# Log gates of a gated linear attention kept as one fp32 array, with fp32 running sums and decay weights built from total minus sum

## The chip, the cores and the metric

The kernel runs on one core of one Trainium2 chip. The metric is the device time of one execution in microseconds, as the median of several runs. The engines are TensorE (PE in the rows; PEld is its weight load), VectorE (DVE), ScalarE (ACT), GpSimd (POOL) and SyncE (SP, which here only issues transfers).

## The reference, cut to what matters

One layer of a backbone over 512 latent tokens, width 1024, with 256 context tokens in front. Of the layer, this case touches the gated linear attention (GLA) branch: 4 heads, key width 128, value width 256, run over the tokens forwards and backwards. For each direction there is a log gate per token and key channel, and the state is decayed by it:

```python
def log_gate(lr, up, bias):
    pre = (lr @ up + bias).astype(jnp.float32)
    return heads(jax.nn.log_sigmoid(pre) / GLA_TAU, GLA_DK)
...
b = jnp.cumsum(gi, axis=1)
b_last = b[:, -1]
...
S_new = jnp.exp(b_last)[..., None] * S + jnp.einsum(
    'bshk,bshv->bhkv', ki * jnp.exp(b_last[:, None] - b), vi)
```

The context tokens give only a start state for each direction, with the same weighting of the keys: `k * exp(b[:, -1:] - b)`. The other branch (a state-space scan, SSD), the merge, the output projection and a SwiGLU block follow, and are not changed.

## The kernel before, in words

Tokens stand in six tiles of 128: four of the latent stream, two of the context. Every large product of the layer is done as three products in fp32r (a matmul format of reduced precision): each weight block is loaded in fp32 (`raw_...`, three buffers in rotation, issued on SP's queue), split into a high part by ACT (`whi_...`, line 188) and a remainder by DVE or POOL (`wlo_...`, line 189), and multiplied as high times high, high times low and low times high. `some_ada` slips a modulation block between them: it is loaded through the same three buffers and summed by POOL (lines 341 to 345).

The order of instructions on each engine is laid down when the program is built: a planner simulates the engines and places each instruction by when it expects it to be ready. Instructions issued through `Early` (the matmuls and transposes of the chains) or under `high_priority` go ahead of others. On the chip, each engine then runs its list in that order and waits where an input is late.

**The gates** (lines 466 to 480). For 2 directions times 6 token tiles, PE forms `pre` in [token, channel]; ACT does three passes over 128x512 (absolute value, exponential, logarithm), and DVE one (line 474), which leaves the log gate `ge`. Then DVE rounds it to fp32r (`gh`, line 477) and forms the remainder (`gl`, line 478), and both go by SP's queue to a DRAM array `gdr`. Around these lines in time stand the value and gate projections of head 0 (`r_v`, `r_r`) on PE, the time steps of the SSD branch (`dtT`, `dt_...`, `cum`, `suf`, `cumT`, lines 488 to 567), which run as a chain through PE, DVE and ACT, and the query and key projections of head 1 (`l_q`, `l_k`).

**The chain of a GLA head** (`gla_chain`, once for each of 4 heads). For each direction, POOL's queue loads the head's columns of `gh` and `gl` (`g`, line 592). With 0/1 triangle matrices (`mkr`) PE forms three things, each as a pair of products with the high and the low part: the running sums in [channel, token] for the four latent tiles (`gc`, line 598), the suffix sums in [token, channel] for three latent tiles (`kx`) and for two context tiles (`ky`). ACT exponentiates the suffix sums (lines 613, 614) and DVE multiplies them with `kt`, the keys in [token, channel] (lines 615, 616), which gives the weighted keys `kd`. `kt` was made in `gla_proj_qk` by six transposes of the keys `kT` (line 441) and two copies (line 442). Then the states `S` are formed from `kd` and the values, the within-tile attention in seven levels (`eq`, `ek`, `lv`, `att`), and at the end the outputs `o`, which need `S` and `att`.

PE works on the projections of head h+1 while the chain of head h runs. Results of the chain pass through four PSUM banks in rotation (`sm_bank`); `g` and `kd` of one direction take turns in two buffers (tags `cva`, `cvt`).

Of the kernel before, what the change touches and what calls it, by code (L numbers as in the profile page):

```python
# [24 lines left out]
DK = 128  # L25
# [4 lines left out]
TAU = 16.0  # L30
# [13 lines left out]
M_ID, M_LE, M_GE, M_GT, M_LT, M_ONE = range(6)  # L44
# [85 lines left out]
def hybrid_layer_kernel(ctx: ExitStack, tc: tile.TileContext, x, xc, wts, vec, rows, up, msk, lvl, out):  # L130
    nc = tc.nc
# [8 lines left out]
    sml = ctx.enter_context(tc.tile_pool(name="sml", bufs=2))  # L140
    ps = ctx.enter_context(tc.tile_pool(name="ps", bufs=4, space=PSUM))
    dr = ctx.enter_context(tc.tile_pool(name="dr", bufs=1, space=DRAM))
# [4 lines left out]
    def sm_bank(name):  # L147
        return ps.tile([P, 512], F32, tag="sm", name=name)
# [4 lines left out]
    mkr = cst.tile([P, 5, P], F32R, name="mkr")  # L153
# [6 lines left out]
    ident = idt[:, :]  # L160
# [64 lines left out]
    with tc.tile_pool(name="st", bufs=1) as st:  # L225
# [77 lines left out]
        for i in range(6):  # L303
# [5 lines left out]
            for half in range(2):  # L309
                pt = sm_bank(f"xT_{i}_{half}")  # L310
                for k in range(4):
                    kk = half * 4 + k
# [7 lines left out]
    pj = mix.enter_context(tc.tile_pool(name="pj", bufs=2))  # L320
    ch = mix.enter_context(tc.tile_pool(name="ch", bufs=1))
# [105 lines left out]
    def gla_proj_qk(h):  # L427
        lat, _ = proj_cols(("q", h), False)
        qT = pj.tile([P, SEQ], F32, tag="p3", name=f"qT_{h}")
        nc.scalar.activation(qT, lat, AF.Copy, scale=float(DK) ** -0.5)  # L430
        big = pj.tile([P, 3072], F32, tag="x12", name=f"kv_{h}")
        vt = big[:, 0:1536].rearrange("p (i c) -> p i c", c=DV)
        kt = big[:, 1536:2304].rearrange("p (i c) -> p i c", c=DK)
        kT = big[:, 2304:3072]
        lat, cx = proj_cols(("k", h), True)
        nc.scalar.activation(kT[:, 0:SEQ], lat, AF.Copy)
        nc.vector.tensor_copy(kT[:, SEQ:NT], cx[:, 0:CTX])
        for b, i0, n in ((0, 0, 4), (1, 4, 2)):
            pt = sm_bank(f"kt_{h}_{b}")
            for i in range(n):  # L440
                nc.tensor.transpose(pt[:, i * P:(i + 1) * P], kT[:, (i0 + i) * P:(i0 + i + 1) * P], ident)
            nc.scalar.activation(kt[:, i0:i0 + n, :], pt[:, 0:n * P].rearrange("p (i c) -> p i c", c=DK), AF.Copy)
        return qT, vt, kt, kT

    def gla_proj_vr(h, qT, vt, kt, kT):
        banks = proj_rows(lambda kh: ("v", h, kh), 6)
        for b in range(3):
            nc.scalar.activation(vt[:, 2 * b:2 * b + 2, :], banks[b].rearrange("p (i c) -> p i c", c=DV), AF.Copy)
        banks = proj_rows(lambda kh: ("r", h, kh), 4)
        rw = pj.tile([P, 4, DV], F32, tag="p4", name=f"rw_{h}")  # L450
        for b in range(2):
            rv = rw[:, 2 * b:2 * b + 2, :]
            pv = banks[b].rearrange("p (i c) -> p i c", c=DV)
            with tc.issue_after(ln_end.ins) if h == 0 else nullcontext():
                nc.scalar.activation(rv, pv, AF.Tanh, scale=0.5)
            nc.vector.scalar_tensor_tensor(rv, rv, 1.0, pv, ALU.add, ALU.mult)
            nc.gpsimd.tensor_tensor(rv, rv, gnh.unsqueeze(1).to_broadcast([P, 2, DV]), ALU.mult)
        return qT, vt, kt, kT, rw

    def gla_proj(h):  # L460
        return gla_proj_vr(h, *gla_proj_qk(h))


    gdr = dr.tile([P, 2, 2, 6, 512], F32, name="gdr")

    for d in range(2):
        for i in range(6):
            pt = sm_bank(f"pre_{d}_{i}")
            nc.tensor.matmul(pt, MS[d][:, i * P:(i + 1) * P], U[:, d, :], start=True, stop=True)
            e = ch.tile([P, 512], F32, tag="s2", name=f"ge_{d}_{i}", bufs=7)  # L470
            nc.scalar.activation(e, pt, AF.Abs)
            nc.scalar.activation(e, e, AF.Exp, scale=-1.0)
            nc.scalar.activation(e, e, AF.Ln, bias=1.0)
            nc.vector.scalar_tensor_tensor(e, pt, 0.0, e, ALU.min, ALU.subtract)
            gh = ch.tile([P, 512], F32R, tag="z", name=f"gh_{d}_{i}", bufs=4)
            gl = ch.tile([P, 512], F32R, tag="E4", name=f"gl_{d}_{i}", bufs=4)
            nc.vector.tensor_copy(gh, e)
            nc.vector.tensor_tensor(gl, e, gh.bitcast(F32), ALU.subtract)
            nc.sync.dma_start(gdr[:, d, 0, i, :], gh.bitcast(F32))
            nc.sync.dma_start(gdr[:, d, 1, i, :], gl.bitcast(F32))  # L480


    dsh = [P, 6, 64]
# [1 line left out]
    for b, i0, n in ((0, 0, 4), (1, 4, 2)):  # L485
        pt = sm_bank(f"dtT_{b}")
# [9 lines left out]
    e = dt_tile("dt_e")  # L496
# [63 lines left out]
    for d in range(2):  # L560
        pt = sm_bank(f"cumT_{d}")
# [17 lines left out]

    early = Early()  # L580

    def gla_chain(h, qT, vt, kt, kT, rw, oH, oL):
        def s2(name, shape=(P, SEQ)):
            return ch.tile(list(shape), F32, tag="s2", name=f"{name}_{h}", bufs=7)

        cm, kd = [], []
        for d, mc, ms, n0, far, near in ((0, M_LE, M_GT, 0, 4, 5), (1, M_GE, M_LT, 1, 5, 4)):
            tag = ("cva", "cvt")[d]
            gp = []
            for p_ in range(2):  # L590
                gd = pj.tile([P, 6, DK], F32R, tag=tag, name=f"g_{h}_{d}_{p_}")
                nc.gpsimd.dma_start(gd, gdr[:, d, p_, :, h * DK:(h + 1) * DK])
                gp.append(gd)

            pt = sm_bank(f"gc_{h}_{d}")
            for n in range(NCH):
                for p_ in range(2):
                    early.matmul(pt[:, n * P:(n + 1) * P], gp[p_][:, n, :], mkr[:, mc - 1, :], start=(p_ == 0), stop=(p_ == 1))
            c_ = s2(f"gcum{d}")
            nc.scalar.activation(c_, pt, AF.Copy, scale=1.0 / TAU)  # L600
            cm.append(c_)

            px = sm_bank(f"kx_{h}_{d}")
            for p_ in range(2):
                early.matmul(px[:, 0:384], mkr[:, ms - 1, :], gp[p_][:, n0:n0 + 3, :], start=(p_ == 0), stop=(p_ == 1))
            py = sm_bank(f"ky_{h}_{d}")
            o0 = (far - 4) * P
            for p_ in range(2):
                early.matmul(py[:, 0:256], mkr[:, ms - 1, :], gp[p_][:, 4:6, :], start=(p_ == 0), stop=False)
            for p_ in range(2):  # L610
                early.matmul(py[:, o0:o0 + P], mkr[:, M_ONE - 1, :], gp[p_][:, near, :], start=False, stop=(p_ == 1))
            kk = pj.tile([P, 5, DK], F32, tag=tag, name=f"kd_{h}_{d}")
            nc.scalar.activation(kk[:, 0:3, :], px[:, 0:384].rearrange("p (i c) -> p i c", c=DK), AF.Exp, scale=1.0 / TAU)
            nc.scalar.activation(kk[:, 3:5, :], py[:, 0:256].rearrange("p (i c) -> p i c", c=DK), AF.Exp, scale=1.0 / TAU)
            nc.vector.tensor_tensor(kk[:, 0:3, :], kk[:, 0:3, :], kt[:, n0:n0 + 3, :], ALU.mult)
            nc.vector.tensor_tensor(kk[:, 3:5, :], kk[:, 3:5, :], kt[:, 4:6, :], ALU.mult)
            kd.append(kk)

        qd = []
# [595 lines left out]
```

## Time and profile before

| what | value |
|---|---|
| median of 3 runs | 1433.0 us (1431.25 to 1437.1) |
| the profiled execution | 1428.55 us |
| its span, first to last instruction | 1426.7 us |
| mean granted TensorE clock | 0.986 of full speed |
| PE busy | 1349.4 us, 95% of the span |
| DVE / ACT / POOL busy | 881.1 / 496.7 / 476.1 us |
| DMA | 175.49 MB, mean 123 GB/s |

All rows are of the profiled execution, in microseconds from the start of its span. Busy times of PE overlap, since matmuls are pipelined: what one costs is read from the distance between starts, or from the chain of waits, and not from its duration.

### The profile page before, as it was taken

To read this page: it belongs to the slowest core of one execution; us is meant where nothing else is said; L and a number is where in the kernel's file an instruction comes from. 1 tells how busy PE (TensorE), PEld (TensorE's weight loads), DVE (VectorE), ACT (ScalarE), POOL (GpSimd) and SP (SyncE) were. 2 spreads that over 40 slices of the span, in tenths; PEclk is the share of its full clock that TensorE was granted. 3 is DMA by queue.
4 is the path that set the end of the run, shared out by engine and by line. 5 is a ranking of instruction groups with operands and counts; after the bars stand their busy time and mean duration, and the time that the engine had idled before them with its cause. 6 is when DMAs were issued, how large, how long until landed. Compare 5 with 4: busy or idle time off the path is not lost.

```text
span 1426.7 us, 19130 instructions
## 1 busy us (share of the span) xinstructions
PE 1349.4 (95%) x7462; PEld 1146.0 (80%) x7462; DVE 881.1 (62%) x1317; ACT 496.7 (35%) x825; POOL 476.1 (33%) x341
## 2 busy tenths in 40 slices
PE   5888999999998999998999989999889999999997
PEld 3687999889888778876887787778678888888886
DVE  4599757583595588558857975767683343433235
ACT  6464343433434132532332342332333323232222
POOL 1346555245423533343353324114641122100001
PEclk9998999999999999999999999999999999999999
DMA  9375433423422423323322333457423343333331
GB/s 370 123 259 151 128 102 111 126 93 126 122 75 67 141 98 101 97 73 90 104 82 89 96 97 101 158 184 267 135 87 109 113 122 115 120 116 93 100 106 72
DMA packets 71386, 175.49 MB, mean 123 GB/s; under 512 B 6384, under 2 KB 22912, under 8 KB 71168
## 3 DMA queue, kind: packets, MB, share of 16 engines
q1 hardware_dynamic: 57056, 161.11, 34.6%
q0 software_dynamic: 13952, 12.79, 3.8%
q8 instruction: 59, 0.97, 0.3%
q10 hardware_dynamic: 288, 0.36, 0.1%
q14 instruction: 31, 0.25, 0.1%
HBM read 159.37 MB, written 14.87 MB: 122 GB/s over the span
## 4 chain that ended last, share of the span: by engine, by line
PE 66%; DVE 16%; DMA 9%; issue 5%; ACT 2%; POOL 1%; SPq 0%; POOLq 0%; DVEq 0%; ACTq 0%
DMA E<-cdr 6%; PE up L1069 3%; PE gate L1068 3%; PE gate L1069 3%; PE up L1068 3%; PE gate L1067 3%; PE up L1067 3%; DVE E L830 3%; PE db L204 3%; PE db L206 3%; PE db L205 3%; PE lv L577 2%; PE pb_pb L716 2%; PE pb_pb L715 2%; PE pb_pb L717 2%
## 5 line engine op out<-in xcount | busy, mean ns | idle before, releaser
L341 POOL TENSOR_TENSOR raw_ada<-raw_ada,cs 128x1024 f32<-128x1024 f32 x32 | 69.7, 2180 | 265.3 <-DMA raw_ada<-in_wts_dram 230.4
L830 DVE TENSOR_TENSOR E<-E,ebias 128x512 f32<-128x512 f32 x64 | 68.8, 1077 | 51.0 <-DMA E<-cdr 50.8
L343 POOL TENSOR_TENSOR raw_ada<-raw_ada 128x512 f32<-128x512 f32 x64 | 80.0, 1250 | 3.7
L386 PE MATMUL r_z<-whi_z,hH 128*128 128x256 f32 x256 | 74.6, 291 | 5.8 <-DVE z L781 3.0
L388 PE MATMUL r_z<-whi_z,hL 128*128 128x256 f32 x256 | 73.4, 287 | 0.0
L387 PE MATMUL r_z<-wlo_z,hH 128*128 128x256 f32 x256 | 73.0, 285 | 0.0
L1067 PE MATMUL gate<-h2H,whi_gate 128*128 128x512 f32 (+1 forms) x192 | 72.2, 376 | 0.0
L1068 PE MATMUL gate<-h2L,whi_gate 128*128 128x512 f32 (+1 forms) x192 | 72.1, 376 | 0.0
L1069 PE MATMUL gate<-h2H,wlo_gate 128*128 128x512 f32 (+1 forms) x192 | 71.9, 374 | 0.0
L189 POOL TENSOR_TENSOR wlo_xs<-raw_xs,whi_xs 128x1024 fp32r<-128x1024 f32 x16 | 40.6, 2536 | 75.3 <-ACT whi_xs L188 75.3
L1069 PE MATMUL up<-h2H,wlo_up 128*128 128x512 f32 x160 | 63.0, 394 | 0.0
L1068 PE MATMUL up<-h2L,whi_up 128*128 128x512 f32 x160 | 62.4, 390 | 0.0
L1067 PE MATMUL up<-h2H,whi_up 128*128 128x512 f32 x160 | 62.3, 389 | 0.0
L189 DVE TENSOR_TENSOR wlo_down<-raw_down,whi_down 128x1024 fp32r<-128x1024 f32 x18 | 22.1, 1225 | 62.4 <-ACT whi_down L188 62.3
L189 DVE TENSOR_TENSOR wlo_gate<-raw_gate,whi_gate 128x1024 fp32r<-128x1024 f32 x20 | 31.7, 1584 | 45.6 <-ACT whi_gate L188 45.6
L170 POOL TENSOR_TENSOR rr_f<-rv_f,negh 128x1 f32<-128x1 f32 x4 | 2.6, 662 | 168.5 <-DVE rv_f L168 168.5
L386 PE MATMUL r_v<-whi_v,hH 128*128 128x256 f32 x192 | 56.4, 294 | 0.0
L189 POOL TENSOR_TENSOR wlo_z<-raw_z,whi_z 128x1024 fp32r<-128x1024 f32 x16 | 39.6, 2475 | 49.2 <-ACT whi_z L188 36.6
L387 PE MATMUL r_v<-wlo_v,hH 128*128 128x256 f32 x192 | 55.5, 289 | 0.0
L715 PE MATMUL pb_pb<-yT,whi_pb 128*128 128x512 f32 x128 | 55.3, 434 | 0.0
L388 PE MATMUL r_v<-whi_v,hL 128*128 128x256 f32 x192 | 55.3, 288 | 0.0
L205 PE MATMUL db<-wlo_down,fH 128*128 128x512 f32 x142 | 55.3, 389 | 0.0
(479 smaller groups left out, 4446.7 us busy)
## 6 DMA issues: line engine op xcount, KB each, us to landing
raw_ada<-in_wts_dram SPq DMA_DIRECT2D x32, 512.0 KB, 4.0
E<-cdr SPq DMA_DIRECT2D x64, 256.0 KB, 3.5
raw_gate<-in_wts_dram SPq DMA_DIRECT2D x22, 512.0 KB, 3.7
raw_up<-in_wts_dram SPq DMA_DIRECT2D x22, 512.0 KB, 3.5
raw_down<-in_wts_dram SPq DMA_DIRECT2D x22, 512.0 KB, 3.5
aw<-in_wts_dram SPq DMA_DIRECT2D x8, 1024.0 KB, 15.5
raw_xs<-in_wts_dram SPq DMA_DIRECT2D x16, 512.0 KB, 3.5
raw_z<-in_wts_dram SPq DMA_DIRECT2D x16, 512.0 KB, 3.6
```

The lines of the kernel that those rows point to most:

```text
L189: (nc.gpsimd if split_pool[0] else nc.vector).tensor_tensor(lo, raw, hi.bitcast(F32), ALU.subtract)
L205: nc.tensor.matmul(out_, aH, bL, start=False, stop=False)
L341: nc.gpsimd.tensor_tensor(raw, raw, cs[:, :, 0:1].to_broadcast([P, KD, P]), ALU.mult)
L343: nc.gpsimd.tensor_tensor(raw[:, 0:n, :], raw[:, 0:n, :], raw[:, n:2 * n, :], ALU.add)
L386: nc.tensor.matmul(o, hH[:, kk, tk], hi[:, k, :], start=st, stop=False, skip_group_check=True)
L387: nc.tensor.matmul(o, hH[:, kk, tk], lo[:, k, :], start=False, stop=False, skip_group_check=True)
L388: nc.tensor.matmul(o, hL[:, kk, tk], hi[:, k, :], start=False, stop=sp, skip_group_check=True)
L715: nc.tensor.matmul(pt, hi[:, k, cl], aH[:, k, :], start=(k == 0), stop=False)
L830: nc.vector.tensor_tensor(ed, ed, ebias[:, d, n, hh].unsqueeze(2).to_broadcast([P, EH, P]), ALU.add)
L1067: nc.tensor.matmul(pts[kj][:, tk], hi[:, k, :], h2H[:, k, tk], start=(k == 0), stop=False)
L1068: nc.tensor.matmul(pts[kj][:, tk], hi[:, k, :], h2L[:, k, tk], start=False, stop=False)
L1069: nc.tensor.matmul(pts[kj][:, tk], lo[:, k, :], h2H[:, k, tk], start=False, stop=(k == KD - 1))
```

## The change

`gh` and `gl` and their 24 transfers are dropped: `ge` itself is written to `gdr`, which is half as large. Each direction of a head loads one tile `gd` in place of two. The running sums are formed by one fp32 product in place of two fp32r products, for the four latent tiles (`gc`) and now for the two context tiles too (`gx`), all in [channel, token]. The suffix sums `kx` and `ky` are dropped. The weights are exp(total - sum), with the total as a per-channel bias of the exponential, so the five tiles take one exponential each; for the context, two small DVE operations (`tx`) make the bias. The weights are multiplied with `kT` in [channel, token], the five products are transposed on PE (`pk`), and copied by ACT into `kd`. The transposes and copies that made `kt` are dropped.

```diff
-        kt = big[:, 1536:2304].rearrange("p (i c) -> p i c", c=DK)
...
-        for b, i0, n in ((0, 0, 4), (1, 4, 2)):
-            pt = sm_bank(f"kt_{h}_{b}")
-            for i in range(n):
-                nc.tensor.transpose(pt[:, i * P:(i + 1) * P], kT[:, (i0 + i) * P:(i0 + i + 1) * P], ident)
-            nc.scalar.activation(kt[:, i0:i0 + n, :], pt[:, 0:n * P].rearrange("p (i c) -> p i c", c=DK), AF.Copy)
...
-    gdr = dr.tile([P, 2, 2, 6, 512], F32, name="gdr")
+    gdr = dr.tile([P, 2, 6, 512], F32, name="gdr")
...
-            gh = ch.tile([P, 512], F32R, tag="z", name=f"gh_{d}_{i}", bufs=4)
-            gl = ch.tile([P, 512], F32R, tag="E4", name=f"gl_{d}_{i}", bufs=4)
-            nc.vector.tensor_copy(gh, e)
-            nc.vector.tensor_tensor(gl, e, gh.bitcast(F32), ALU.subtract)
-            nc.sync.dma_start(gdr[:, d, 0, i, :], gh.bitcast(F32))
-            nc.sync.dma_start(gdr[:, d, 1, i, :], gl.bitcast(F32))
+            nc.sync.dma_start(gdr[:, d, i, :], e)
...
-            gp = []
-            for p_ in range(2):
-                gd = pj.tile([P, 6, DK], F32R, tag=tag, name=f"g_{h}_{d}_{p_}")
-                nc.gpsimd.dma_start(gd, gdr[:, d, p_, :, h * DK:(h + 1) * DK])
-                gp.append(gd)
-
+            gd = pj.tile([P, 6, DK], F32, tag=tag, name=f"g_{h}_{d}")
+            nc.gpsimd.dma_start(gd, gdr[:, d, :, h * DK:(h + 1) * DK])
+
+            mask = mkr[:, mc - 1, :].bitcast(F32)
+            px = sm_bank(f"gx_{h}_{d}")
+            for n in range(2):
+                early.matmul(px[:, n * P:(n + 1) * P], gd[:, 4 + n, :], mask, start=True, stop=True)
             pt = sm_bank(f"gc_{h}_{d}")
             for n in range(NCH):
-                for p_ in range(2):
-                    early.matmul(pt[:, n * P:(n + 1) * P], gp[p_][:, n, :], mkr[:, mc - 1, :], start=(p_ == 0), stop=(p_ == 1))
+                early.matmul(pt[:, n * P:(n + 1) * P], gd[:, n, :], mask, start=True, stop=True)
...
-            px = sm_bank(f"kx_{h}_{d}")
-            for p_ in range(2):
-                early.matmul(px[:, 0:384], mkr[:, ms - 1, :], gp[p_][:, n0:n0 + 3, :], start=(p_ == 0), stop=(p_ == 1))
-            py = sm_bank(f"ky_{h}_{d}")
-            o0 = (far - 4) * P
-            for p_ in range(2):
-                early.matmul(py[:, 0:256], mkr[:, ms - 1, :], gp[p_][:, 4:6, :], start=(p_ == 0), stop=False)
-            for p_ in range(2):
-                early.matmul(py[:, o0:o0 + P], mkr[:, M_ONE - 1, :], gp[p_][:, near, :], start=False, stop=(p_ == 1))
+
+            col = P - 1 if d == 0 else 0
+            tx = sml.tile([P, 2], F32, tag="gtx", name=f"gtx_{h}_{d}")
+            at = lambda i: px[:, (i - 4) * P + col:(i - 4) * P + col + 1]
+            nc.vector.tensor_scalar(tx[:, 0:1], at(near), 1.0 / TAU, None, ALU.mult)
+            nc.vector.scalar_tensor_tensor(tx[:, 1:2], at(far), 1.0 / TAU, tx[:, 0:1], ALU.mult, ALU.add)
+            ek = pj.tile([P, 5, P], F32, tag=tag, name=f"kw_{h}_{d}")
+            for i, bias in ((near, tx[:, 0:1]), (far, tx[:, 1:2])):
+                nc.scalar.activation(ek[:, i - 1, :], px[:, (i - 4) * P:(i - 3) * P], AF.Exp, bias=bias, scale=-1.0 / TAU)
+            for i in range(3):
+                t0 = (n0 + i) * P
+                nc.scalar.activation(ek[:, i, :], c_[:, t0:t0 + P], AF.Exp, bias=c_[:, t0 + col:t0 + col + 1], scale=-1.0)
             kk = pj.tile([P, 5, DK], F32, tag=tag, name=f"kd_{h}_{d}")
-            nc.scalar.activation(kk[:, 0:3, :], px[:, 0:384].rearrange("p (i c) -> p i c", c=DK), AF.Exp, scale=1.0 / TAU)
-            nc.scalar.activation(kk[:, 3:5, :], py[:, 0:256].rearrange("p (i c) -> p i c", c=DK), AF.Exp, scale=1.0 / TAU)
-            nc.vector.tensor_tensor(kk[:, 0:3, :], kk[:, 0:3, :], kt[:, n0:n0 + 3, :], ALU.mult)
-            nc.vector.tensor_tensor(kk[:, 3:5, :], kk[:, 3:5, :], kt[:, 4:6, :], ALU.mult)
+            for i, n, t0 in ((3, 2, SEQ), (0, 3, n0 * P)):
+                ev = ek[:, i:i + n, :]
+                nc.vector.tensor_tensor(ev, ev, kT[:, t0:t0 + n * P].rearrange("p (i t) -> p i t", t=P), ALU.mult)
+                pk = sm_bank(f"kd_{h}_{d}_{i}")
+                for j in range(n):
+                    early.transpose(pk[:, j * P:(j + 1) * P], ek[:, i + j, :], ident)
+                nc.scalar.activation(kk[:, i:i + n, :], pk[:, 0:n * P].rearrange("p (i c) -> p i c", c=DK), AF.Copy)
             kd.append(kk)
```

## Rows read from the trace of the kernel before

**Rows 1.** The page's busy times: busy us, share, instructions.

```profile
PE 1349.4 (95%) x7462; PEld 1146.0 (80%) x7462; DVE 881.1 (62%) x1317; ACT 496.7 (35%) x825; POOL 476.1 (33%) x341
```

**Rows 2.** Stretches: busy us of PE, PEld, DVE, ACT, POOL; then granted clock, DMA share.

```profile
74.80:92.60 17.80, 17.77 (x141) 17.20 (x139) 17.73 (x24) 14.62 (x28) 9.46 (x8) 1.00 0.81 285
92.60:109.20 16.60, 10.34 (x83) 9.63 (x81) 16.50 (x23) 4.20 (x8) 8.88 (x10) 0.95 0.97 276
109.20:125.00 15.80, 13.78 (x59) 11.83 (x60) 14.16 (x23) 7.99 (x14) 8.84 (x8) 0.73 0.66 193
125.00:430.00 305.00, 301.04 (x1976) 275.98 (x1974) 205.97 (x357) 115.32 (x210) 141.18 (x103) 1.00 0.38 110
```

**Rows 3.** Waits of PE, 55 to 125: total us, times, longest.

```profile
PE l_q L366 <- DVE wlo_q L189: 3.3, 1, 3.3
PE dtT L488 <- DVE ge L474: 2.7, 1, 2.7
PE kt L441 <- DVE cumT L564: 2.0, 1, 2.0
```

**Rows 4.** DVE groups, 74.5 to 109: count, busy us, mean ns, idle before.

```profile
L478 DVE TENSOR_TENSOR gl<-ge,gh 128x512 fp32r<-128x512 f32 x12 | 15.8, 1328 | 0.1
L477 DVE CAST gh<-ge 128x512 fp32r<-128x512 f32 x12 | 8.5, 713 | 0.1
```

**Rows 5.** Timeline of ACT and DVE, 88 to 109: start, us, operation.

```profile
88.66 0.62 ACT L473 ACTIVATE ge<-ge 128x512 f32<-128x512 f32 x1
...
93.11 1.16 ACT L473 ACTIVATE ge<-ge 128x512 f32<-128x512 f32 x2
...
95.80 1.22 DVE L189 TENSOR_TENSOR wlo_r<-raw_r,whi_r 128x1024 fp32r<-128x1024 f32 x1
...
103.06 0.53 ACT L497 ACTIVATE dt_e<-dt_v 128x384 f32<-128x384 f32 x1 [8.79 <-DVE dt_v L489]
...
107.94 1.22 DVE L189 TENSOR_TENSOR wlo_q<-raw_q,whi_q 128x1024 fp32r<-128x1024 f32 x1
```

**Rows 6.** Chain of waits, 109 to 131: start, us on the chain.

```profile
110.01 0.43 PE l_q L361
...
115.01 0.24 PE l_q L362
...
120.98 1.05 PE kt L441 x4
...
128.55 0.23 PE ky L577 x2
...
129.58 0.62 PE gc L577 x6
130.20 0.28 PE l_k L366
```

**Rows 7.** Timeline of PE: eight records of four fp32 products.

```profile
163.41 1.06 PE L577 MATMUL lv<-eq,ek 128*128 128x128 f32 x8
164.23 0.37 PE L388 MATMUL r_v<-whi_v,hL 128*128 128x256 f32 x1
```

**Rows 8.** ACT groups by form: copies of 128x128, biased passes of 128x256.

```profile
L838 ACT ACTIVATE cbs<-cb 128x128 f32<-128x128 f32 x16 | 4.3, 271 | 13.6 <-PE cb L577 13.6
...
L740 ACT ACTIVATE cv_x<-c_xs,vecs 128x256 f32<-128x256 f32 x13 | 7.2, 555 | 0.0
```

**Rows 9.** DVE group by form: one column out of PSUM.

```profile
L215 DVE TENSOR_TENSOR ada<-ada,vecs 128x1 f32<-128x1 f32 x19 | 2.9, 152 | 12.5 <-PE ada L336 12.4
```

**Rows 10.** Transfers, 60 to 130: us from issue to landing.

```profile
raw_q<-in_wts_dram SPq DMA_DIRECT2D x1, 512.0 KB, 5.9
```

**Rows 11.** States and outputs of the heads: ns min/median/max, first and last start.

```profile
L577 PE MATMUL S<-kv,kd x80: 377/379/432, 133.6 to 390.0; 128*128 128x256 f32 x80
...
L577 PE MATMUL o<-S,qd x64: 377/380/484, 172.7 to 435.6; 128*128 128x256 f32 x64
```

**Rows 12.** Waits of PE, 125 to 440: total us, times, longest.

```profile
PE lv L577 <- DVE ek L667: 2.6, 4, 1.7
```

More of the change, by code (lines that the diff above doesn't have):

```diff
@@ L437, in gla_proj_qk, with gla_proj_vr @@
         nc.vector.tensor_copy(kT[:, SEQ:NT], cx[:, 0:CTX])
-        for b, i0, n in ((0, 0, 4), (1, 4, 2)):
-            pt = sm_bank(f"kt_{h}_{b}")
-            for i in range(n):
-                nc.tensor.transpose(pt[:, i * P:(i + 1) * P], kT[:, (i0 + i) * P:(i0 + i + 1) * P], ident)
-            nc.scalar.activation(kt[:, i0:i0 + n, :], pt[:, 0:n * P].rearrange("p (i c) -> p i c", c=DK), AF.Copy)
-        return qT, vt, kt, kT
-    def gla_proj_vr(h, qT, vt, kt, kT):
+        return qT, vt, kT
+    def gla_proj_vr(h, qT, vt, kT):
         banks = proj_rows(lambda kh: ("v", h, kh), 6)
@@ L457, in gla_proj_vr @@
             nc.gpsimd.tensor_tensor(rv, rv, gnh.unsqueeze(1).to_broadcast([P, 2, DV]), ALU.mult)
[L458 removed]
+        return qT, vt, kT, rw
     def gla_proj(h):
         return gla_proj_vr(h, *gla_proj_qk(h))
[L464 removed]
+    gdr = dr.tile([P, 2, 6, 512], F32, name="gdr")
     for d in range(2):
@@ L580, in hybrid_layer_kernel, with gla_chain @@
     early = Early()
-    def gla_chain(h, qT, vt, kt, kT, rw, oH, oL):
+    def gla_chain(h, qT, vt, kT, rw, oH, oL):
         def s2(name, shape=(P, SEQ)):
@@ L586, in gla_chain @@
         cm, kd = [], []
-        for d, mc, ms, n0, far, near in ((0, M_LE, M_GT, 0, 4, 5), (1, M_GE, M_LT, 1, 5, 4)):
+        for d, mc, n0, far, near in ((0, M_LE, 0, 4, 5), (1, M_GE, 1, 5, 4)):
             tag = ("cva", "cvt")[d]
-            gp = []
-            for p_ in range(2):
-                gd = pj.tile([P, 6, DK], F32R, tag=tag, name=f"g_{h}_{d}_{p_}")
-                nc.gpsimd.dma_start(gd, gdr[:, d, p_, :, h * DK:(h + 1) * DK])
-                gp.append(gd)
+            gd = pj.tile([P, 6, DK], F32, tag=tag, name=f"g_{h}_{d}")
[4 more added lines that the diff above has]
+                early.matmul(px[:, n * P:(n + 1) * P], gd[:, 4 + n, :], mask, start=True, stop=True)
             pt = sm_bank(f"gc_{h}_{d}")
             for n in range(NCH):
-                for p_ in range(2):
-                    early.matmul(pt[:, n * P:(n + 1) * P], gp[p_][:, n, :], mkr[:, mc - 1, :], start=(p_ == 0), stop=(p_ == 1))
+                early.matmul(pt[:, n * P:(n + 1) * P], gd[:, n, :], mask, start=True, stop=True)
             c_ = s2(f"gcum{d}")
```

## The prediction

> **What bounds the kernel now.** I read the page first: PE is busy for 95% of the span [rows 1], so a change counts if it takes work from PE, or a wait that PE sits through. Then I cut the first third into stretches, since everything that the diff touches lies there. The reader is to see three regimes [rows 2]. From 74.8 to 92.6 PE and DVE are both full. From 92.6 to 109.2 DVE stays full, 16.50 of 16.60 us, while PE falls to 10.34: DVE sets the pace, and ACT with 4.20 is idle. From 109.2 to 125 PE's granted clock is 0.73 in the mean. From 125 to 430, where the four heads' chains run, PE is full again, 301.04 of 305, with DVE at two thirds and ACT at 38%.
>
> The waits of PE name what it stands for in the weak stretch: 2.7 us for a gate pass of DVE (line 474) before the transposes `dtT`, 3.3 us for DVE's split of the next query weights, 2.0 us for DVE's copy of `cumT` [rows 3]. All three are DVE running late, not long operations in themselves. The groups of DVE show what it runs late with: `gl` and `gh`, 24 instructions, 24.3 us of the 34.5 us from 74.5 to 109 [rows 4]. The timeline shows how that passes on [rows 5]: ACT's last gate logarithm ends at 94.3, but ACT starts the time steps' first pass only at 103.06, after 8.79 us of waiting for DVE, and the split `wlo_q` comes at 107.94. So the change removes the work of the engine that PE waits for here. That is the case for a gain; the case for its size is below.
>
> **The change part by part.**
>
> *The split of the gates.* Removed: 12 casts and 12 subtractions on DVE, 24.3 us, and half of the gate transfers. DVE's backlog when ACT is through with the gates is from 94.3 to about 107, some 13 us, less than the 24.3 us that go, so DVE would keep up with ACT. What is late next? The gates then end with ACT, whose three passes do not get shorter: the last ends at 94.3 as now. The bank that `dtT` waits for is freed by the gate pass after the logarithm of 88.66 [rows 5], so at about 90, before PE comes to it at 92.5: the 2.7 us go. The time steps' chain starts on ACT at about 94.3 in place of 103.06. `wlo_q` needs its raw buffer, freed by `wlo_r` (95.80 now, from about 91 when DVE is free), a transfer of 5.9 us [rows 10], and some 2.3 us of splitting: ready at about 99.5 to 103.5, the later end if SP's queue still holds the block up behind a modulation block. PE, without its first stall, comes to it at about 102. So the 3.3 us go, or at the worst 1.5 of them stay.
>
> What the idle time costs beyond itself is seen on the chain of waits: `l_q` products take 0.43 us each from 110.01 on and 0.24 at 115.01 [rows 6]. Ten run at the long distance; 10 x 0.19 = 1.9 us. Four `kt` transposes take 1.05 us where 0.41 would be the full-speed price, another 0.6. The granted clock in that stretch is between the level of 2.4 GHz and that of 1.2 [rows 2], and what stood ahead of the slow products is the 3.3 us wait. Without the wait I expect them at 2.4 GHz.
>
> Sum: 2.7 + 3.3 + 1.9 + 0.6 + 2.0 = 10.5 us at most. I take the first three in full, 7.9, and half of the last two, 1.3, since the wait for `cumT` belongs to a chain through PE, DVE and ACT that starts 8.8 us earlier, but PE comes to it about as much earlier too. That is **9.2 us**, with ends of 2.7 (only the first wait goes) and 10.5.
>
> *PE's products.* Before, one head and direction takes 14 fp32r products, 1.65 us on the chain, from the first `ky` at 128.55 to the `l_k` at 130.20, all of them inside [rows 6]. Eight times that is 13.2 us; 24 `kt` transposes at 0.10 add 2.4: 15.6. After, there are six fp32 products. An fp32 product is two records in this trace: the four products of one level are eight records, and take 163.41 to 164.23, 0.82 us, 0.205 each [rows 7]. Six are 1.23; five transposes at one record's price, 0.10, are 0.51. Eight times 1.74 is 13.9. So PE's work falls by **1.7 us**. A transpose could cost up to 0.26, as the slow `kt` row has it; then the 40 after cost 6.4 us more and the 24 before 3.8, and the balance here is +0.9 instead of -1.7. I take 0.10, because that row lies in the slow stretch.
>
> Of this price the rows say that an fp32r product of 128 columns takes 0.103 us, six `gc` in 0.62 [rows 6], so a pair costs as much as one fp32 product. The Trainium skill (FP8 and Floating Point Precision, section TensorE Precision Notes) has true fp32 as four passes through the array, against one read at reduced precision. By that rule alone a pair would be two passes and its fp32 successor four, and the running sums would double in cost; the trace shows the four-pass price (0.205) but not the cheap pair.
>
> *The path to `kd`.* New on it, for each direction: two one-column operations on DVE at 0.15 [rows 9], five exponentials of 128x128 with a bias on ACT, and five transposes, 0.51. Nothing before shows such an exponential. The nearest are a 128x128 copy, 0.27, and a 128x256 pass with pointer bias and scale, 0.56 [rows 8]; I take 0.27, the same shape, and 0.56 as the upper end. The two copies out of PSUM at the end stand for the two wide exponentials of before, shape for shape. So the path grows by 0.3 + 1.36 + 0.51 = 2.2 us per direction, up to 3.6: over eight, 17.3 to 29 us of latency. What covers it: the first `S` starts at 133.6 and the first `o`, which needs it, at 172.7 [rows 11], and in the whole stretch PE waits 2.6 us for the levels [rows 12]. I charge **1 us**, with 0 and 29 as ends. As engine time it adds 40 x 0.27 = 10.8 us to ACT and 16 x 0.15 = 2.4 to DVE; ACT has 190 us free there and DVE 99 [rows 2], so both cost nothing as long as PE has projections to run.
>
> *Buffers and queues.* POOL issues eight gate loads fewer, each of which stood in its queue among the modulation sums. Tags `cva` and `cvt` still take three tiles per direction, but the next head's load now waits for transposes instead of `S`, so it can start earlier. I price both at nothing: PE does not wait for POOL in [rows 3] or [rows 12], so there is nothing to gain, and with less work in POOL's queue nothing to lose.
>
> **The sum.** 9.2 + 1.7 - 1.0 = 9.9 us, against the profiled execution's 1428.55: 1418.65. The median of the runs stands 4.45 above that execution, so 1433.0 - 9.9 = **1423.1 us**. From 430 on nothing is changed, and I expect it to be shifted as a whole.
>
> **The rivals.**
>
> *A new wait takes the old one's place (no change).* DVE's backlog goes, but PE then stands for the time steps (`cum`, `cumT`), for ACT or for a raw block. For it: ACT is 14.62 of 17.80 busy in the gate stretch and cannot end sooner. Against it: 8.79 us of ACT's waiting is on DVE alone. Then only the 2.7 and the 1.7 come: 1428.6, within 0.5%.
>
> *The longer path to `kd` decides (slower).* The banks of `S`, `dg` and `lv` follow the new transposes' banks in a rotation of four, so the levels stand behind both directions' paths; and the projections of the head after next, which could fill PE, need the buffers that this head frees last. If the growth is exposed in all eight, at a price midway between 17.3 and 29, it is 23 us against a gain of 10.9: 1445. It decides once more than 18 us are exposed. Against it: 39 us between first `S` and first `o`, and a total wait of 2.6 us.
>
> *PE's work rises instead of falling (no change).* If the pairs cost by their columns, the 14 products are 2560 columns, five times 512, at 0.23 each 1.15 us in place of 1.65, and the balance is 15.6 - 8 x 0.5 = 11.6 before against 13.9 after: +2.3 for -1.7. Then the gain is 5.9, and the time 1427.1. Against it: the 1.65 and the 0.103 are read directly. The rule of the skill named above points this way.
>
> **Chances and range.** The gain of the start-up, mostly or wholly: 0.64. A new wait in its place: 0.20. The longer path: 0.11. Dearer products: 0.05. A measurement of this kernel tells about 0.5%, 7.2 us, from no change. Faster by more than that takes the first case: 0.64; within it the second and fourth, and part of the third, where the path eats just the gain: 0.28; slower 0.08. Low end: the whole 10.5, the 1.7 and the 2.6 us of waits for the levels make 14.8, so 1418, and 3 us for the spread of the runs gives 1415. High end: the second rival at 1428.6 and about as much spread gives 1431. Left out are most of the third case and some misjudged extreme below.
>
> **What would show it.** Right: no `gl` and `gh` on DVE; from about 93 to 109 PE near full and DVE not; `dt_e` starting at 94 to 96; no wait of `l_q` on `wlo_q`; `l_q` products at 0.23 throughout; the first `l_k` product of head 1 about 10 us before 121.7; `gc` and `gx` as twelve records in about 1.23 us; the same length from there to the end. Wrong: a new wait of PE of 3 us or more between 90 and 125; waits of `S`, `dg` or `lv` on ACT's copies into `kd` or on the transposes, in each head; ACT late with `whi` splits; or a stage past 430 that grows, since the order of all engines is planned anew.

## The result and the profile after

The change makes the kernel slower: 1456.1 us against 1434.1, ratio 1.0165 (95% interval 1.0139 to 1.0190; four runs of each, side by side). The forecast was 1423.1, the range 1415 to 1431. Each kernel of the experiments below was timed beside the kernel before too (4 to 10 runs of it, 15 to 25 of the kernel before, whose median moves between 1433.1 and 1434.1).

The page of the profiled execution after gives a span of 1453.1 us, 26.4 more than before (the medians are 22.0 apart; some 4 us are the spread between executions). Its busy times (us, share, instructions):

```profile
PE 1360.2 (94%) x7462; PEld 1148.8 (79%) x7462; DVE 884.4 (61%) x1309; ACT 507.0 (35%) x857; POOL 457.9 (32%) x333
```

VectorE lost `gh` and `gl`, 24.3 us [rows 4], and yet its total did not fall, 884.4 for 881.1 [rows 1]: other passes take longer, most of all the sixteen that normalise `y` in the SSD stages, far from the change. Before and after (count, busy us, mean ns, idle before):

```profile
L866 DVE SCALAR_TENSOR_TENSOR y<-y,rr_y,snw 128x512 f32<-128x512 f32 x16 | 11.9, 745 | 3.4 <-POOL rr_y L170 3.4
L861 DVE SCALAR_TENSOR_TENSOR y<-y,rr_y,snw 128x512 f32<-128x512 f32 x16 | 24.6, 1535 | 5.6 <-POOL rr_y L170 5.6
```

The ninth experiment comes back to them. The stretches of [rows 2], same columns:

```profile
74.80:92.60 17.80, 17.80 (x144) 17.45 (x143) 9.43 (x13) 14.85 (x28) 8.82 (x7) 1.00 0.69 223
92.60:109.20 16.60, 15.65 (x108) 14.15 (x106) 9.10 (x16) 4.26 (x8) 10.61 (x11) 1.00 0.70 218
109.20:125.00 15.80, 9.65 (x43) 8.34 (x44) 9.99 (x15) 6.90 (x12) 9.30 (x8) 0.68 0.43 136
125.00:430.00 305.00, 296.87 (x1943) 270.04 (x1942) 211.47 (x369) 124.15 (x242) 118.20 (x94) 0.99 0.30 97
```

From 74.8 to 109.2 the engines' shares came as forecast: DVE falls from full to about half, and PE rises to 15.65 of 16.60. The third line undoes it: PE is busy for 9.65 of 15.80 us, where it was 13.78, at a clock of 0.68. The waits of PE from 55 to 125 (total, times, longest) name the new one:

```profile
PE cum L522 <- ACT dt_aH L516: 6.4, 1, 6.4
...
PE l_q L366 <- DVE wlo_q L189: 0.7, 1, 0.7
```

Both old waits of [rows 3], 2.7 for `dtT` and 3.3 for `wlo_q`, are gone or down to 0.7, and one of 6.4 us stands for the time steps. The timeline of ACT (start, us, operation, in brackets the idle time and what ended it) shows why they are late; its last line is of the kernel before:

```profile
93.18 1.16 ACT L467 ACTIVATE ge<-ge 128x512 f32<-128x512 f32 x2
100.99 1.06 ACT L188 ACTIVATE whi_q<-raw_q 128x1024 fp32r<-128x1024 f32 x1 [6.65 <-DMA raw_q<-in_wts_dram]
101.95 0.51 ACT L486 ACTIVATE dt_e<-dt_v 128x384 f32<-128x384 f32 x1
...
110.87 1.06 ACT L188 ACTIVATE whi_k<-raw_k 128x1024 fp32r<-128x1024 f32 x1 [6.55 <-DMA raw_k<-in_wts_dram]
111.83 0.51 ACT L505 ACTIVATE dt_ln<-dt_u 128x384 f32<-128x384 f32 x1
...
111.84 0.52 ACT L516 ACTIVATE dt_ln<-dt_u 128x384 f32<-128x384 f32 x1 [3.86 <-DVE dt_u L515]
```

Before these two steps ACT no longer waits for DVE, but its list has the copies `whi_q` and `whi_k` ahead of `dt_e` and `dt_ln`, and it stands twice for a weight block, 13.2 us together. So `dt_ln` starts when it did before, 111.83 for 111.84. The blocks are late because SP cannot issue them sooner: its queue waits for a raw buffer that POOL's modulation sum still holds (waits of SP, 75 to 125):

```profile
SPq L176 <- POOL apr L345: 20.5, 5, 5.7
```

Where the rest of the 26.4 us went is read from four stretches between the same instructions in both traces: first `l_bm` of SSD group 0 to that of group 1, on to the first `ob`, to the first `db`, to the first `db_last`. Before:

```profile
362.40:494.20 131.80, 127.41 (x763) 110.69 (x761) 87.86 (x149) 50.98 (x92) 50.15 (x26) 1.00 0.29 86
494.20:992.20 498.00, 474.52 (x2594) 390.98 (x2593) 361.53 (x550) 165.45 (x282) 173.24 (x113) 1.00 0.37 119
992.20:1299.10 306.90, 296.08 (x1394) 247.45 (x1393) 145.08 (x153) 92.85 (x126) 82.31 (x54) 0.98 0.37 116
1299.10:1414.70 115.60, 115.60 (x511) 95.79 (x510) 39.13 (x47) 26.83 (x34) 1.55 (x2) 1.00 0.29 92
```

After:

```profile
366.20:502.50 136.30, 130.11 (x770) 112.09 (x769) 96.22 (x157) 53.33 (x102) 44.91 (x23) 0.99 0.25 79
502.50:1012.70 510.20, 477.88 (x2593) 394.58 (x2592) 365.17 (x544) 166.72 (x282) 174.79 (x112) 0.99 0.35 115
1012.70:1321.80 309.10, 297.43 (x1395) 247.17 (x1394) 153.28 (x156) 93.51 (x128) 83.79 (x55) 0.98 0.37 117
1321.80:1440.80 119.00, 119.00 (x512) 95.88 (x511) 39.32 (x47) 26.72 (x34) 1.55 (x2) 1.00 0.28 89
```

Of the 26.4 us, 3.8 arise up to the first `l_bm` (366.2 for 362.4), all the rest behind it, in code that the diff does not touch: 4.5, 12.2, 2.2, 3.4, and 0.3 at the end. The 3.8 are within the spread: in the traces of the first, third and fourth experiments, whose work up to there is that of the kernel before, the first `l_bm` starts at 369.1, 364.5 and 369.1. Two things are to be seen. In the second stretch PE does the same matmuls (2593 for 2594 records) but is idle for 32.3 us in place of 23.5. In the last it is never idle in either trace and takes 119.0 for 115.6 us over the same 510 products, one every 0.2333 us in place of 0.2267.

The waits of PE say what it stands for in the second stretch. Before, 494.2 to 992.2:

```profile
PE yT L577 <- DVE y L866: 9.8, 6, 1.9
...
PE r_z L386 <- DVE z L781: 3.0, 2, 1.6
```

After, 502.5 to 1012.7:

```profile
PE yT L566 <- DVE y L861: 15.9, 9, 3.1
PE r_z L386 <- DVE z L776: 4.8, 3, 2.6
PE tr_x L752 <- ACT bt L753: 3.4, 3, 1.5
PE c_xs L364 <- DVE rv_y L168: 2.5, 1, 2.5
```

The same kinds of wait, longer and more, with two new ones. DVE has no more to do there (544 instructions for 550, 365.2 us for 361.5), so it does the same things in another order. The planner, which lays the lists of all engines anew, had indeed built different lists.

### The profile page after: what moved, and what is told of

The parts are those of the page before. It is cut to its first block, busy times and chain, and to the rows that moved or that the text cites. A ratio compares the mean times of both kernels' runs of the same rounds, so it can differ in the third digit from the quotient of the medians.

```text
span 1453.1 us, 19099 instructions
## 1 busy us (share of the span) xinstructions
PE 1360.2 (94%) x7462; PEld 1148.8 (79%) x7462; DVE 884.4 (61%) x1309; ACT 507.0 (35%) x857; POOL 457.9 (32%) x333
## 4 chain that ended last, share of the span: by engine, by line
PE 51%; DVE 14%; DMA 6%; issue 5%; POOL 2%; ACT 2%; SPq 0%; POOLq 0%; DVEq 0%; ACTq 0%
DMA E<-cdr 4%; PE db L205 3%; PE up L1064 3%; PE db L204 3%; PE db L206 3%; PE up L1063 3%; PE up L1062 3%; PE gate L1063 3%; PE gate L1064 3%; PE gate L1062 3%; DVE E L825 2%; PE pb_pb L710 2%; PE pb_pb L711 2%; PE pb_pb L712 2%; PE r_z L386 1%
## 5 line engine op out<-in xcount | busy, mean ns | idle before, releaser
L341 POOL TENSOR_TENSOR raw_ada<-raw_ada,cs 128x1024 f32<-128x1024 f32 x32 | 64.3, 2010 | 275.8 <-DMA raw_ada<-in_wts_dram 236.7
L825 DVE TENSOR_TENSOR E<-E,ebias 128x512 f32<-128x512 f32 x64 | 53.1, 834 | 48.8 <-DMA E<-cdr 48.8
L343 POOL TENSOR_TENSOR raw_ada<-raw_ada 128x512 f32<-128x512 f32 x64 | 74.8, 1169 | 4.0
L386 PEld LDWEIGHTS r_z<-whi_z,hH 128*128 128x128 f32 x256 | 49.9, 196 | 7.8 <-DVE z L776 5.6
L206 PE MATMUL db<-whi_down,fL 128*128 128x512 f32 x142 | 56.0, 394 | 0.0
```

The costliest lines, as they stand in the source:

```text
L206: nc.tensor.matmul(out_, aL, bH, start=False, stop=stop)
L341: nc.gpsimd.tensor_tensor(raw, raw, cs[:, :, 0:1].to_broadcast([P, KD, P]), ALU.mult)
L343: nc.gpsimd.tensor_tensor(raw[:, 0:n, :], raw[:, 0:n, :], raw[:, n:2 * n, :], ALU.add)
L386: nc.tensor.matmul(o, hH[:, kk, tk], hi[:, k, :], start=st, stop=False, skip_group_check=True)
L825: nc.vector.tensor_tensor(ed, ed, ebias[:, d, n, hh].unsqueeze(2).to_broadcast([P, EH, P]), ALU.add)
```

## The experiments

Three suspects: the **order** of the SSD stages, the **addresses** (the new tile `gtx` moves every SBUF tile allocated behind it by 64 bytes per partition), and the **work** of the change itself, with its two parts.

**1. Addresses alone.** The kernel before with one small tile that nothing uses:

```diff
+    sml.tile([P, 2], F32, tag="gtx", name="pad16", bufs=2)
```

> The kernel before with an unused two-column buffer in the small pool, so that every later SBUF tile starts 64 bytes higher, as in the changed kernel; each engine's list of instructions stays the same. Theory: the place in SBUF alone makes the products of the last stage (db, 512 columns) start every 0.233 us in place of 0.227, over some 520 products 3.4 us: about 1437.5. Rival: the place does not matter, and the changed kernel's slower db products come from elsewhere (a lower clock, data): 1434, products at 0.227.

Measured: 1436.1 us, ratio 1.0022 (1.0004 to 1.0040). The stretch from the first `db` to the first `db_last`:

```profile
1308.30:1427.30 119.00, 119.00 (x511) 95.88 (x510) 39.29 (x47) 26.79 (x34) 1.55 (x2) 1.00 0.27 89
```

The instruction lists are those of the kernel before, and the 3.4 us of the last stretch come back to the tenth. By the medians the addresses alone are worth 2.0 us (1436.1 - 1434.1); the rest of the loss is not theirs.

**2 to 4. The order.** From the first SSD projection on, each engine's list was tied to a stored list, by dependences that set an order and no wait:

```diff
+    pin_start = len(nc.cur_bb.bb.instructions)
     split_pool[0] = True
     sp = ssd_proj(0)
...
+    ins = list(nc.cur_bb.bb.instructions)[start:]
+        for a, b in zip(order[:-1], order[1:]):
+            tc.add_manual_dep(ins[b], ins[a].name, mybir.DependencyInfo(mybir.DependencyClass.NoSync, mybir.DependencyReason.DATA),
+                              reason="pinned order")
```

Second kernel: the changed one with the list of before, and `gtx` in a buffer of the existing tile `gam`, which puts the addresses back.

> The changed kernel, its small tile put into an existing buffer so that all later tiles stand where they stood before, and the instructions from the first SSD projection to the end tied, on each engine, to the order that they have in the kernel before. Theory: most of the loss lies in the order that the planner gave the unchanged SSD stages; from 494 on before (502 after) they lost 16 us, and the layout 3.4: about 1436 to 1438. Rival: the loss there comes with the change itself (later inputs, transfers, a state of the chip) whatever the order: 1450 to 1453.

Measured: **1425.6 us, ratio 0.9953 (0.9935 to 0.9972)**, 30.5 below the changed kernel and faster than the kernel before. That is lower than the theory's 1436 to 1438, by some 10 us.

Third: the kernel before with the list of the changed one.

> The converse: the kernel before, unchanged in its work and layout, with the instructions from the first SSD projection on tied to the order that they have in the changed kernel. Theory of the order: about 1448 to 1452, the SSD stages 14 to 16 us longer. Rival, the order does not matter or only together with the new chain: 1434.

Measured: 1446.9, ratio 1.0102 (1.0066 to 1.0139), just below the theory's 1448 to 1452.

Fourth, the control: the kernel before tied to its own list.

> Control: the kernel before, with the same stretch tied to its own order. Nothing but a few places among the last GLA head's instructions differ. Every theory: 1434, within 2 us. If it is off by more, tying itself has a price, and the two other tied runs are read against this one.

Measured: 1433.9, ratio 1.0008 (0.9987 to 1.0028): the tie costs nothing. So the order costs 13.0 us (1446.9 - 1433.9) even where not an instruction of the change is present. From the first `l_bm` to the first `ob`, with the list of before (fourth) and of the changed kernel (third):

```profile
369.10:1000.00 630.90, 605.65 (x3354) 505.38 (x3353) 447.06 (x698) 216.80 (x374) 224.58 (x138) 0.99 0.35 111
364.50:1007.10 642.60, 609.01 (x3355) 509.88 (x3354) 453.58 (x696) 217.76 (x373) 220.55 (x137) 0.98 0.35 109
```

**5. Order without addresses.** The changed kernel with `gtx` in `gam`'s buffer, no tie.

```diff
-            tx = sml.tile([P, 2], F32, tag="gtx", name=f"gtx_{h}_{d}")
+            tx = sml.tile([P, HPG], F32, tag="gam", name=f"gtx_{h}_{d}")
```

> The changed kernel with only its SBUF addresses put back (the 2-column tile gtx takes a buffer of an existing tile); its orders stay as they are. If layout and order add up (layout 3.4 us by the run that moved the addresses alone): 1452 to 1453 us, and the last stage, from the first db product to db_last, back from 119.0 to 115.6 us, with the SSD stages still about 16 us longer than before. Rival: the addresses are behind most of the loss (order and addresses work together): 1440 us or less.

Measured: 1450.3, ratio 1.0102 (1.0083 to 1.0120). The last stretch is back at 115.60, the stretch from the second group to `ob` stays long:

```profile
499.50:1012.40 512.90, 482.87 (x2592) 399.91 (x2591) 362.89 (x545) 166.94 (x282) 173.89 (x112) 0.97 0.36 114
1321.30:1436.90 115.60, 115.60 (x512) 95.72 (x511) 39.15 (x47) 26.73 (x34) 1.55 (x2) 1.00 0.28 91
```

By the medians the addresses are worth 5.8 us here (1456.1 - 1450.3) and were 2.0 in the first experiment; both traces show 3.4 in the last stretch, and the differences from that are about the spread of the runs.

**6, 7. The two parts, tied.** Each part alone, with the order of before from the first SSD projection on. The gates alone (one fp32 array, fp32 products, suffix sums and `kt` as before):

```diff
-                for p_ in range(2):
-                    early.matmul(pt[:, n * P:(n + 1) * P], gp[p_][:, n, :], mkr[:, mc - 1, :], start=(p_ == 0), stop=(p_ == 1))
+                early.matmul(pt[:, n * P:(n + 1) * P], gd[:, n, :], mask(mc), start=True, stop=True)
...
+            early.matmul(px[:, 0:384], mask(ms), gd[:, n0:n0 + 3, :], start=True, stop=True)
```

> The kernel before with the first part of the change alone: gates as one fp32 array and fp32 products for the three sums; k's transposes and the suffix sums stay; order from the first SSD projection on tied to the kernel before. Theory: the 8.5 us that the change brings when the order is kept come from the 24 VectorE instructions and 12 stores that go: 1425 to 1427 us. Rival: the new path of the keys brings it (24 transposes and 8 evictions of k less): 1432 to 1434 us.

Measured: 1436.3, ratio 1.0017 (1.0000 to 1.0034). A miss: the part that takes the work off DVE brings nothing by itself.

The keys alone (pairs kept, `gx` formed from pairs, weights from exp(total - sum), five transposes):

```diff
+            px = sm_bank(f"gx_{h}_{d}")
+            for n in range(2):
+                for p_ in range(2):
+                    early.matmul(px[:, n * P:(n + 1) * P], gp[p_][:, 4 + n, :], mkr[:, mc - 1, :], start=(p_ == 0), stop=(p_ == 1))
```

> The kernel before with the second part alone: pairs gh and gl stay, the weighted keys come from exp(total - sum) and are transposed, k's transposes are dropped; order from the first SSD projection on tied to the kernel before. Theory: the longer path to the weighted keys and the PE time saved cancel: 1433 to 1436 us, above the run with the gates alone. Rival: this part brings the gain: 1425 to 1428 us.

Measured: 1446.7, ratio 1.0078 (1.0058 to 1.0098): slower by 12.6 us, more than the theory gave.

**8. The time steps first.** The second kernel with ACT's copies `whi_q` and `whi_k` put behind the steps that they held up:

```diff
+            with tc.issue_after(hold[key].ins) if key in hold else nullcontext():
+                nc.scalar.activation(hi, raw, AF.Copy)
...
+    hold[("q", 1)] = nc.scalar.activation(lu, u, AF.Ln)
...
+    hold[("k", 1)] = nc.scalar.activation(aH, a, AF.Copy)
```

> The changed kernel with addresses and later order of the kernel before (1425.6 us), and on ScalarE the time-step chain (dt_e to dt_aH) put ahead of the copies of the weights of head 1's q and k, which wait for their loads. Theory: the four heads' chains are serial, so what counts is when the chain of head 0 starts; cum can run some 8 us earlier (107 instead of 115), the first gx at 117 to 119 instead of 125, each later oT 5 to 8 us earlier, the whole 1417 to 1421 us. Rival: PE's own work up to 440 us is the bound, or the chain is held by what follows the cum: 1424 to 1427 us.

Measured: 1430.9, ratio 0.9991 (0.9974 to 1.0008): above the second kernel, so neither theory. The first `gx` did come at 117.5 in place of 125.3, but the first `oT` of head 0 stays where it was, 198.3 in both. PE in 50 to 125 and 125 to 362, for this kernel:

```profile
50.00:125.00 75.00, 69.85 (x452) 63.06 (x451) 51.96 (x75) 46.13 (x80) 40.42 (x32) 0.93 0.50 157
125.00:362.00 237.00, 223.51 (x1483) 207.25 (x1484) 148.99 (x266) 89.68 (x179) 101.09 (x83) 0.96 0.30 98
```

and its waits of PE in the second of the two:

```profile
PE oT L569 <- DVE on L693: 9.5, 4, 4.1
PE kd L569 <- DVE kw L610: 3.7, 1, 3.7
```

PE's idle time (length less busy) falls to 5.2 us in the start-up and rises to 13.5 in the head chains. In the kernel before the two are 12.5 and 2.5, after the change 11.3 and 7.3, in the second kernel 9.4 and 7.6: the sum is 15.0, 18.6, 17.0, and here 18.6. What the start-up saves, the chains of the heads take back; but how 1.6 us more of idle time than in the second kernel go with 5.3 us more in the median is not shown.

**9. What tips the order over.** The lists can be compared without a chip. Of the pairs of neighbours in VectorE's list from the first SSD projection on, these shares stand together in the list of before, and in that of the changed kernel:

```
                                                 before  changed
changed kernel                                     0.52    1.00
before, 8 gate loads less (one a head, direction)  0.53    0.98
before, 2 gate loads less (head 3 alone)           0.53    0.98
changed, head 0's, 1's or 2's gates loaded twice   0.52    1.00
changed, head 3's gates loaded twice               0.91    0.50
keys alone                                         0.91    0.50
```

So two transfers out of eight, the second loads of head 3, tip the plan with nothing else of the change present, and the new path of the keys does not. The ninth kernel, with the addresses of before and no tie, has them back:

```diff
             nc.gpsimd.dma_start(gd, gdr[:, d, :, h * DK:(h + 1) * DK])
+            if h == 3:
+                nc.gpsimd.dma_start(gd, gdr[:, d, :, h * DK:(h + 1) * DK])
```

> The changed kernel with the addresses of before, no order tied; head 3's gates are loaded twice, one after the other, into the same tile: two transfers more (one per direction), no result of which is new. With them the planner lays out the SSD stages almost as in the kernel before. Theory: the loss of the change is in the plan that it tips over, and the plan was tipped by these two transfers alone: 1425 to 1431 us, the SSD stages (first l_bm to the third l_ga) 518 to 522 us instead of 544. Rival: the loss hangs on the change's own work or on other orders too: 1445 to 1451 us.

Measured: **1432.3, ratio 0.9995 (0.9978 to 1.0011)**, a little above the theory's range and far from the rival's. Two transfers that bring nothing new make the changed kernel 18.0 us faster (1450.3 - 1432.3; 17.0 if each is taken against the kernel before that was timed beside it). The stretch from the second group to `ob`:

```profile
497.80:998.10 500.30, 480.04 (x2613) 395.71 (x2612) 360.45 (x553) 166.34 (x284) 175.81 (x115) 0.99 0.37 119
```

The tenth kernel takes the two from the kernel before:

```diff
+                if h == 3 and p_ == 1:
+                    gp.append(gd)
+                    continue
```

> The kernel before with two transfers less: for head 3 the low parts of the gates aren't loaded, and both products of each sum read the high part (head 3's sums are left wrong by that). Everything else, all products too, stays. Theory: the plan of the SSD stages tips over as in the changed kernel: 1444 to 1450 us, as with the tied order of the changed kernel (1446.9). Rival: 1430 to 1436 us.

Measured: 1445.1, ratio 1.0092 (1.0061 to 1.0122): 12.0 us slower with less to do. The same stretch:

```profile
493.90:1002.50 508.60, 482.01 (x2592) 399.50 (x2591) 360.00 (x544) 166.99 (x282) 174.45 (x112) 0.97 0.36 115
```

**What the other order does** is seen at one place, a normalisation in group 1. In the changed kernel (timelines of POOL and DVE):

```profile
563.47 2.33 POOL L189 TENSOR_TENSOR wlo_z<-raw_z,whi_z 128x1024 fp32r<-128x1024 f32 x1
563.53 2.83 DVE L861 SCALAR_TENSOR_TENSOR y<-y,rr_y,snw 128x512 f32<-128x512 f32 x1 [0.40 <-POOL rr_y L170]
```

In the ninth kernel:

```profile
564.97 0.74 DVE L863 SCALAR_TENSOR_TENSOR y<-y,rr_y,snw 128x512 f32<-128x512 f32 x1
...
566.43 2.41 POOL L189 TENSOR_TENSOR wlo_z<-raw_z,whi_z 128x1024 fp32r<-128x1024 f32 x1 [2.81 <-PE yT L566]
```

In the changed kernel's list POOL's split of `z`'s weights stands right behind the root that `y` needs too, so the split and the pass `y` start together, `y` takes 2.83 us, and PE, which needs it for `yT`, stands. In the ninth the split comes after `yT`, and `y` takes 0.74. It is not this place alone. The sixteen passes `y` take 11.9 to 14.1 us in each of the ten traces whose order is that of before or near it, and 20.4 to 24.6 in the four with the other order (after, third, fifth, tenth). From the first `l_bm` to the first `ob` PE's waits for `y` and `z` sum to 9.3 to 12.8 us in the kernel before, the first, second, fourth and ninth, and to 17.3 to 21.6 in those four. Windows of the changed kernel, there and a little later:

```profile
563.00:566.50 3.50, 0.43 (x4) 0.15 (x2) 3.10 (x3) 0.63 (x1) 2.80 (x2) 1.00 0.22 75
...
586.00:592.00 6.00, 1.93 (x15) 1.49 (x13) 2.97 (x7) 3.76 (x8) 0.00 (x0) 1.00 0.40 131
592.00:596.00 4.00, 4.00 (x24) 4.00 (x23) 3.15 (x7) 3.49 (x7) 1.23 (x1) 0.58 0.00 0
```

From 586 to 592 PE is busy for 1.93 us of 6 (it waits for `bt` and `z`), and behind that the granted clock is 0.58, a mixture of the two levels, 1.2 and 2.4 GHz, though PE is full again. A wait can thus cost its own length and a piece of slow work after it. The ninth kernel has such places too, but its idle time in the stretch is 20.3 us (500.3 - 480.04) against 30.0 in the fifth (512.9 - 482.87).

**11, 12. The two parts, without a tie.** The gates alone with head 3's gates loaded three times (here the list stays near that of the changed kernel with two loads, so the count is no rule), and the keys alone as they are:

```diff
+            if h == 3:
+                nc.gpsimd.dma_start(gd, gdr[:, d, :, h * DK:(h + 1) * DK])
+                nc.gpsimd.dma_start(gd, gdr[:, d, :, h * DK:(h + 1) * DK])
```

> The gates alone (one fp32 array, fp32 products), no order tied; head 3's gates are loaded three times, so that the plan of the SSD stages stays near that of before. If this part alone is worth nothing, as with the tied order (1436.3): 1432 to 1437 us. If the tie cost the gain: 1424 to 1428 us.

Measured: 1437.8, ratio 1.0036 (1.0023 to 1.0048): no gain without the tie either.

> The new path of the keys alone, pairs gh and gl kept, no order tied (the plan of the SSD stages stays near that of before by itself). If the path to the keys is what costs, as with the tied order (1446.7; first S of a head 15 to 26 us after its first sum instead of 8 to 11): 1443 to 1449 us. If the tie or the plan cost it: 1433 to 1437 us.

Measured: 1445.5, ratio 1.0091 (1.0073 to 1.0109). Both agree with the tied runs, so the tie is not behind the two misses. In the traces of the keys alone, tied and not, the first `l_bm` starts at 379.2 and 378.2, against 362.4 to 369.1 with the work of before: the loss lies in the heads' chains. First and last start of the states `S`, in the gates alone:

```profile
L572 PE MATMUL S<-kv,kd x80: 377/378/462, 134.1 to 404.4; 128*128 128x256 f32 x80
```

in the keys alone:

```profile
L571 PE MATMUL S<-kv,kd x80: 377/379/463, 149.1 to 413.4; 128*128 128x256 f32 x80
```

and in the changed kernel:

```profile
L566 PE MATMUL S<-kv,kd x80: 377/379/483, 141.4 to 393.8; 128*128 128x256 f32 x80
```

Before it was 133.6 [rows 11]. The path to the keys shows: 7.2 us from the first sum (126.9) to the first state with the gates alone, 10.2 before (123.4), 15.0 after (126.4), 25.7 with the keys alone (123.4).

## Why the prediction was wrong

**The step that failed** is "From 430 on nothing is changed, and I expect it to be shifted as a whole." 22.6 of the 26.4 us arise behind the first `l_bm`, at 362 to 366. Two causes were shown. The order: the changed kernel loses 17.0 to 18.0 us to it by the ninth kernel, and the kernel before, with nothing else of the change, loses 12.0 to 13.0 by the third and tenth; why it is more with the change is not shown. The addresses: 2.0 to 5.8 us by the medians, 3.4 in the last stretch of the traces. What is left for the work of the change itself is small: 0.8 us faster in the ninth kernel, 8.5 in the second (1434.1 - 1425.6). The second is near the 9.9 that were forecast, but not by the steps that were forecast, as the next paragraph shows: so far as it agrees, that is luck. The text had named a stage past 430 that grows, since the order of all engines is planned anew, as what would show it wrong, but gave it no chance and no price. Behind that stood a step on queues: the eight gate loads were priced "at nothing" because PE waits for none of them. No wait of PE after the change names POOL's queue, so that much holds; in the plan two of the eight decide.

**The start-up, 9.2 us, is the second step that failed.** Its first half came: no backlog on DVE, and the waits for `ge` and `wlo_q` gone or down to 0.7. But `dt_e` started at 101.95, where 94 to 96 was forecast, and PE's idle time from 50 to 125 fell by 1.2 us alone, from 12.5 to 11.3 (to 9.0 to 9.4 in the second, fifth and ninth kernels). By the first `l_bm` nothing of a gain is left: the four kernels with the whole change come to it at 365.1 to 366.8, the four with the work of before at 362.4 to 369.1. The rival of a new wait in its place is what happened, and where it said, at the time steps; the reading that ACT's 8.79 us were spent on DVE was right, but behind DVE stood the next thing that ACT waits for, the raw blocks, in ACT's own list. With that moved as well (the eighth kernel) 7.3 of the 12.5 us go, near the 8.0 that the three waits sum to, and still the time does not fall: the chains of the heads take it back. In this kernel a wait that PE no longer has would count only if PE had other work later, at the place where the chain makes it wait.

**The path to the keys, charged 1 us.** Mis-sized. The exponentials take 0.37 and 0.40 us (forecast 0.27, upper end 0.56). The keys alone cost 12.4 us (1445.5 - 1433.1), so the rival of the longer path is real, though the whole change does not show it at that price: with the order kept, both parts together stand at 0.9995 or 0.9953. Why the keys cost 12 us alone and not together with the gates was not settled. In the keys alone DVE still carries `gh` and `gl`, and the first state comes 7.7 us later than with both parts; that would fit, but no run tests it. The gates alone bring nothing either (1.0017 and 1.0036).

**PE's products, -1.7 us.** Right in its terms: eight records of `gc` take 0.81 us in the changed kernel, 127.31 to 128.12, as forecast from [rows 7], and two transposes into `kd` 0.22, 133.87 to 134.09. Too small to be seen in the total. The rival of dearer products has nothing behind it.

**ACT and DVE time, nothing.** Right for the engines' shares, wrong in what it hides: a pass of DVE has no fixed length beside POOL (below). The 24.3 us of `gl` and `gh` held such time too: `gl` takes 1.33 us in the mean [rows 4], but 0.68 at 96.94, with POOL idle.

What stays open: the second kernel (tied, 1425.6) and the ninth (not tied, 1432.3) do the same work at nearly the same order, with 54 us of PE idle each between 50 and the first `db_last`. In the two traces PE is busy for 6.6 us longer in the ninth, at a lower granted clock (0.979 in the mean against 0.988). But the clock does not settle it: over the ten runs of each the clocks overlap (0.982 to 0.988, and 0.979 to 0.985) and the times do not (1423.1 to 1428.3, and 1429.8 to 1435.1). What the 6.7 us between the medians come from was not found.

## What to carry to other kernels

Where a planner or a recording layer lays down the order, an edit in one stage is an edit in all: compare the built lists first, and price a new order of the untouched stages as a case of its own (here 12 to 18 us, more than any term of the sum). To time the edit itself, tie the untouched part to the old order and keep the old addresses; to find what tipped the order, take parts of the edit away until the lists agree, which needs no run. And before a wait is counted as won, ask what the waiting engine's own list holds next, and whether the chain behind it ends any sooner.

## What the runs showed of the hardware

**Addresses.** 64 bytes more per partition make the same 512-column products start every 0.2333 us and not every 0.2267, over 510 products with PE never idle, in the changed kernel and in the first experiment alike, and back at 0.2267 when the addresses are put back (fifth). Why is not shown. The products that end the stage, 256 columns wide, do not become longer: 281 ns where they were 283.

**VectorE beside GpSimd.** Two `coef` passes of VectorE took 0.63 us in the second kernel, with GpSimd idle:

```profile
123.10 0.63 DVE L543 TENSOR_TENSOR coef<-coef,dt 128x192 f32<-128x192 f32 x2
```

and 3.42 us in the eighth, where they fell on GpSimd's modulation sums:

```profile
116.60 1.95 POOL L344 TENSOR_TENSOR raw_ada<-raw_ada,cs 128x1024 f32<-128x1024 f32 x1
116.72 3.42 DVE L546 TENSOR_TENSOR coef<-coef,dt 128x192 f32<-128x192 f32 x2
118.64 1.28 POOL L346 TENSOR_TENSOR raw_ada<-raw_ada 128x512 f32<-128x512 f32 x1
```

So moving the time steps forward put these passes under the sums. That may be a part of why the eighth kernel's chain gained nothing; no run tests it. The Trainium skill (SBUF — State Buffer, section SBUF: two separate sides) says that VectorE and GpSimd share a pair of ports by an exclusive lock, held for the whole instruction, also against VectorE operations with two SBUF inputs while GpSimd's reads SBUF. The trace agrees: `coef` reads two tiles of SBUF, and its two passes end at 118.78 and 120.14, each 0.2 us after one of the sums (118.55 and 119.92). In the changed kernel the pass `y` at 563.53 ends at 566.36, 0.6 us after the split beside it (565.80).
